# Mixture of experts: a fixed order on TensorE, nested conditions for further blocks, one hinted jump

## The chip, the cores and the metric

The kernel runs on one core of a Trainium2 chip. The metric is the device time of one execution in microseconds (us). The engines are TensorE (PE in the rows; its weight loads are PEld), VectorE (DVE), ScalarE (ACT), GpSimd (POOL) and SyncE (SP), which here only issues DMAs. A "q" behind an engine's name means its sequencer: the part that waits, branches and issues.

## What is computed

Two layers of a transformer block: a mixer (RWKV, S5 and windowed attention), a layer norm, a mixture of experts, a layer norm. The change touches the mixture of experts alone:

```python
def hier_moe(h, ...):                       # h: 768 tokens in layer 1, 512 in layer 2, of 1024 features
    ...                                     # each token: a group, two of its 8 experts, two weights
def run_block(inp):                         # a block of tokens of one expert e
    x_blk, e = inp
    return (silu(x_blk @ w_gate[e]) * (x_blk @ w_up[e])) @ w_down[e]
```

There are 32 experts in each layer; w_gate and w_up are 1024 x 512, w_down is 512 x 1024, all in float32, so an expert has 6.29 MB of weights. All 32 are read in each layer, whatever their number of tokens.

## The kernel before

Routing writes a table of the tokens of each expert to DRAM. In `experts` (L1867) a static path takes each expert's first block of 64 tokens; `NB` (L1699) is 3, so a second and a third block stand behind a condition each, and a loop at the end takes what is beyond (L1902). `rt.nov` holds the number of further blocks of each expert.

`tokens_T` (L1734) turns the gathered rows of two experts at once into `xT`: 8 transposes on TensorE (line L59 in the rows, from `xg`, or `xo` for further blocks) and two copies. `ffn_up` (L1749) is the product with gate and the product with up, 16 matmuls each (a float32 matmul shows as two in the trace), then silu on ScalarE (L1758) and the product of both on VectorE (L1759), called `act`. `ffn_down` (L1763) turns `act` by two transposes (L59), copies the result to `aT` on VectorE (L1770), makes the product with down in 8 matmuls (L1775), empties the bank (L1777, on ScalarE in the first layer, on VectorE in the second, where a gate row is multiplied in), and scatters the rows to DRAM from GpSimd (L1778).

The loop is shifted by one: in turn e it makes `ffn_up` of expert e, then, if e is odd, `tokens_T` of the next pair and the gather for a later one, then `ffn_down` of expert c = e - 1, then the conditions of c (L1895). The order on each engine is a scheduler's, not written by hand. Each of the engines TensorE, VectorE, ScalarE and GpSimd reads the number n of c (L1893) and branches for itself; an engine that skips a block still sends the semaphores that the block would have sent.

`Weights` (L1786) keeps three experts' matrices in a ring. SyncE issues the three fetches of expert e + 3 (L1811) when TensorE has passed the conditions of expert e, since the further blocks read the same matrices. `others` (L1853) fetches the tokens of further blocks, under a condition on GpSimd.

Of the kernel before, what the change touches and what calls it, by code (L numbers as in the profile page):

```python
# [10 lines left out]
F32 = mybir.dt.float32  # L11
# [9 lines left out]
D = 1024  # L21
# [9 lines left out]
class K:  # L31
    """the state of the build: engines, pools, constants"""

    def __init__(self, tc, a):
        self.tc, self.nc, self.a = tc, tc.nc, a
        self.dr = {}
        self.win = {}               # split columns of w_in
        self.free = []              # streams to use once instead
        self.stream = ('m', 8)      # the PSUM banks of the code being traced: tag, number
# [6 lines left out]
    def bank(self):  # L46
        """a PSUM bank of the current stream"""
        return self.ps.tile([128, 512], F32, name='b_' + self.stream[0], tag='b_' + self.stream[0], bufs=self.stream[1])

    def pool(self, name, st, **kw):  # L50
        """a pool whose tiles wait for the earlier tiles on their own bytes only"""
        return st.enter_context(self.tc.tile_pool(name=name, bufs=1, reuse_waits="tile", **kw))


def tr(k, out, x):
    """out = x^T on the tensor engine"""
# [5 lines left out]
def row(ap):  # L62
    """a DRAM vector [n] as [1, n]"""
# [18 lines left out]
def rsqrt(k, out, x, eps, p=128):  # L82
    """out = (x + eps)^-0.5 for a small tile"""
# [7 lines left out]
def mod_c(k):  # L91
    """silu of both condition vectors, [128, 8, 32] with d = 8 p + k, columns 0 (lat) and 1 (ctx)"""
# [13 lines left out]
    # b_mod of the first two thirds in columns; shift and 1 + scale of both layers  # L106
# [7 lines left out]
def mod_unit(k, l, mp, c0, n, bufs=2):  # L114
    """columns c0..c0+n of the modulation: the first two vectors to k.cols, the other four as rows to DRAM, 512 columns at a time"""
# [31 lines left out]
# float32 operands of the projection are split exactly into two of the tensor engine's 22-bit floats: x = hi + lo  # L147
def x_turn(k, xr, i, x):
    """columns of token tile i of xr [128, 8, 768], d = 128 k + p, from x [128, 1024]"""
# [7 lines left out]
def x_split(k, l, xT, xr, kk):  # L157
    """rows kk of xT from xr: modulated, split"""
# [11 lines left out]
def ln_rows(k, l):  # L170
    """the affine map of layer l's second norm, feature-major"""
# [6 lines left out]
def ln_cols(k, l, P, gb):  # L178
    """in feature-major columns the affine map gb of layer l's second norm and the next layer's modulation together"""
# [10 lines left out]
def x_tile(k, l, P, xT, i, x, cols):  # L190
    """columns of token tile i of xT from x [128, 1024]: turned, and by what is returned scaled and shifted, split"""
# [22 lines left out]
def win(k, l, pp, at, load=False):  # L214
    """columns 256 at.. of w_in, split; or their load alone"""
# [14 lines left out]
def proj(k, l, pp, xT, sink, tiles, segs=SEGS):  # L230
    """sink(m, c0, psum, n) takes feature tile m (128 features) of n tokens from c0"""
# [18 lines left out]
def rwkv_consts(k):  # L250
    """triangular masks over blocks of 64 tokens, one per direction"""
    nc, c = k.nc, k.cp
    k.cum, k.msk = [], []
    for d in range(2):
        # cum[i, t] = -e^-0.5 where i comes no later than t in the same block
# [6 lines left out]
        # msk[i, (a, r), t]: strictly before, no later  # L262
# [17 lines left out]
def rwkv_weights(k, l, rp, fp):  # L280
    """fp: pool of what only the features take"""
    nc, a = k.nc, k.a
    wa = fp.tile([128, 2, 2, 256], F32, name='wa2')      # w2 and a2, each zero on the other's rows
# [25 lines left out]
def conv_sink(k, P, cv, cvd, m, c0, p, n):  # L309
    """cvd [tile, 128, 8, 128] <- the centred convolution of the feature rows in PSUM"""  # L310
# [8 lines left out]
def to_tiles(k, d, m, c0, n, o, eng=None):  # L319
    """d [tile, 128, m, 128] <- o [128, n], feature tile m, tokens c0..c0+n"""  # L320
# [4 lines left out]
def rwkv(k, l, st, cvd, Y, ys, streams, fill):  # L325
    """cvd [tile, 128, 8, 128] convolved features; ys gets the tiles of the mixer's output, in pool Y, feature-major [128, 2, 128].
    streams: two PSUM streams; fill traces other work between the parts"""
    nc, tc = k.nc, k.tc
    emit_ctx = l == 0
    P = k.pool('rwA', st)       # lives through the chain  # L330
    sS, sF = ExitStack(), ExitStack()
    Q = k.pool('rwS', sS, side='right')     # the inverses
    Fp = k.pool('rwF', sF)      # features and scores of the tiles
    Rp = None                   # the steps
    pb, wa, g2 = rwkv_weights(k, l, P, Fp)
    V, G, A = nc.vector, nc.gpsimd, nc.scalar
    # of the chunk c of tile slot s: what a step takes (kb | v, W | x a | r | scores of r), what the inverse takes (scores of a), a | A_ak v
# [4 lines left out]
    def sigmoid(t):  # L342
        """(1 + tanh(x / 2)) / 2"""
# [7 lines left out]
    inv_o = k.dram('inv_out', [96, 64, 64])     # zero off the diagonal blocks of 32  # L351
    inv_t = k.dram('inv_t', [96, 32, 32])

    # the triangular inverses go in two batches; in each the forward tiles first
# [4 lines left out]
    # v, zero on the rows of b; keys and b of each head of a pair, zero on the rows of the other head  # L359
# [7 lines left out]
    def front(i):  # L367
        """token-major features of tile i"""
# [5 lines left out]
        # the low-rank inputs: tanh(w_lo) | a_lo, the gate's  # L374
# [5 lines left out]
        # decay  # L380
# [5 lines left out]
        # learning rate  # L386
# [5 lines left out]
        rk = Fp.tile([128, 512], F32, name='rk', bufs=2)      # r | k  # L392
# [11 lines left out]
        # unit keys  # L404
# [12 lines left out]
        # the decay of a whole chunk, per key channel  # L417
# [7 lines left out]
        gm = P.tile([128, 8, 2], F32, name='gm%d' % i)        # (d, pair, chunk), head of the pair  # L425
        G.tensor_tensor(gm, gc[:, :, None].to_broadcast([128, 8, 2]), k.hpm[:, None, :].to_broadcast([128, 8, 2]), op=ALU.mult)
        GM[i] = (gc, gm)
        # keys of both directions
# [6 lines left out]
        # a = kk * decay up to the token before  # L435
# [8 lines left out]
        if out:  # L444
            # the bonus
# [11 lines left out]
        for d in range(2):  # L457
            z = slot[i, d]
            # keys and v above, b and W below
# [1776 lines left out]
```

## Time and profile before

| | us |
|---|---|
| three runs | 2976.47, 2986.68, 2986.15 |
| their median | 2986.15 |
| the profiled execution: span from first to last instruction | 2973.4 |
| experts of the first layer, first to last product | 936.2 to 1541.6 |
| experts of the second layer | 2373.4 to 2923.7 |

The profiled execution has no time of its own beside its span; the runs lie 3 to 13 us above it. A row of the profile gives the line, the engine, what is written from what, how often, the busy time, and in brackets the idle time of the engine just before and what ended it. "PEq L1895" as what ended it means that TensorE stood still while its sequencer was at the condition. [...]

### The profile page before, as it was taken

To read this page: it belongs to the slowest core of one execution; us is meant where nothing else is said; L and a number is where in the kernel's file an instruction comes from. 1 tells how busy PE (TensorE), PEld (TensorE's weight loads), DVE (VectorE), ACT (ScalarE), POOL (GpSimd) and SP (SyncE) were. 2 spreads that over 40 slices of the span, in tenths; PEclk is the share of its full clock that TensorE was granted. 3 is DMA by queue.
4 is the path that set the end of the run, shared out by engine and by line. 5 is a ranking of instruction groups with operands and counts; after the bars stand their busy time and mean duration, and the time that the engine had idled before them with its cause. 6 is when DMAs were issued, how large, how long until landed. Compare 5 with 4: busy or idle time off the path is not lost. (4 is left out here: it accounts for less than half of the span.)

```text
span 2973.4 us, 43762 instructions
## 1 busy us (share of the span) xinstructions
PE 2257.8 (76%) x16189; PEld 1533.3 (52%) x16189; DVE 1180.0 (40%) x2830; ACT 522.9 (18%) x1264; POOL 821.5 (28%) x1131
## 2 busy tenths in 40 slices
PE   5898676879775878888864788677797487788882
PEld 3786455667433544555434676455554254454441
DVE  7963455564754000000006873456646611111113
ACT  3222332222001000000014122233120100000001
POOL 2642232331633010111006552333334410011002
PEclk8999677599887999999987898689798699999996
DMA  8334466567547898788865324446783699979994
GB/s 233 94 93 127 141 179 177 152 175 200 178 161 276 337 418 355 307 333 328 328 247 178 83 54 134 116 127 165 222 237 122 258 372 398 390 316 357 365 403 162
DMA packets 404799, 691.40 MB, mean 233 GB/s; under 512 B 134754, under 2 KB 310626, under 8 KB 388096
## 3 DMA queue, kind: packets, MB, share of 16 engines
q1 hardware_dynamic: 311808, 600.10, 56.4%
q10 hardware_dynamic: 78880, 64.32, 7.2%
q0 software_dynamic: 13792, 22.61, 2.1%
q8 instruction: 215, 3.52, 0.5%
q14 instruction: 104, 0.85, 0.1%
HBM read 607.98 MB, written 95.44 MB: 237 GB/s over the span
## 5 line engine op out<-in xcount | busy, mean ns | idle before, releaser
L1756 PE MATMUL b_m<-w,xT 128*64 128x256 f32 x4928 | 605.3, 406 | 145.4 <-PEq L1895 120.2
L1756 PEld LDWEIGHTS b_m<-w,xT 128*64 128x64 f32 x4928 | 431.6, 146 | 340.0 <-issue 125.2
L1759 DVE TENSOR_TENSOR act<-act,b_m 128x256 f32<-128x256 f32 x64 | 26.9, 421 | 751.7 <-PE b_m L1756 751.7
L243 PE MATMUL b_m<-xT,win 128*128 128x256 f32 (+1 forms) x1416 | 273.6, 353 | 8.1 <-POOL xT L167 3.7
L1775 PE MATMUL b_m<-w,aT 128*64 128x512 f32 x1024 | 233.8, 598 | 36.0 <-issue 18.7
L243 PEld LDWEIGHTS b_m<-xT,win 128*128 128x128 f32 x1416 | 230.8, 200 | 41.6 <-POOL xT L167 4.5
L1778 POOL DMA_INDIRECT yb<-y,dx x64 | 63.9, 999 | 630.9 <-DVEq L1895 297.1
L1775 PEld LDWEIGHTS b_m<-w,aT 128*64 128x64 f32 x1024 | 74.3, 136 | 154.3 <-issue 130.1
L1758 ACT ACTIVATE act<-b_m 128x256 f32<-128x256 f32 x64 | 24.5, 383 | 586.3 <-PE b_m L1756 586.2
L877 PE MATMUL b_a<-kz,qb 128*128 128x128 f32 (+2 forms) x416 | 114.9, 423 | 8.6 <-ACT pr L898 5.8
L1582 PE MATMUL b_a<-wo,yt 128*128 128x512 f32 x240 | 112.3, 617 | 0.0
L1842 POOL DMA_INDIRECT xg<-hd,ix x32 | 32.6, 1020 | 248.4 <-PE b_m L59 187.5
L877 PEld LDWEIGHTS b_a<-kz,qb 128*128 128x128 f32 x416 | 79.3, 240 | 32.9 <-issue 13.6
L127 PE MATMUL b_a<-wmod,cc 128*32 128x128 f32 x1280 | 65.4, 320 | 40.1 <-DMA wmod<-in_w_mod_dram 29.9
L59 PE MATMUL b_a<-idf,pr 128*128 128x128 f32 x320 | 59.1, 307 | 35.8 <-DVE pt L921 11.6
L503 PE MATMUL b_g<-ar,bz 128*128 128x128 f32 (+1 forms) x384 | 69.2, 348 | 8.0 <-ACT bz L495 8.0
L503 PEld LDWEIGHTS b_g<-ar,bz 128*128 128x128 f32 x384 | 63.9, 255 | 18.7 <-ACT bz L495 14.6
L1582 PEld LDWEIGHTS b_a<-wo,yt 128*128 128x128 f32 x240 | 45.3, 196 | 51.2 <-issue 50.3
L1777 DVE TENSOR_TENSOR y<-b_m,gate 128x512 f32<-128x512 f32 x32 | 22.1, 691 | 120.8 <-PE b_m L1775 120.8
L127 PEld LDWEIGHTS b_a<-wmod,cc 128*32 128x32 f32 x1280 | 38.3, 123 | 58.2 <-DMA wmod<-in_w_mod_dram 32.7
L551 POOL TENSOR_TENSOR tl<-Bm,Xh 112x4 f32<-112x4 f32 (+13 forms) x112 | 37.8, 337 | 103.0 <-DVE Xh L552 58.9
L59 PEld LDWEIGHTS b_a<-idf,pr 128*128 128x128 f32 x320 | 38.8, 154 | 45.3 <-DVE pt L921 13.7
(539 smaller groups left out, 3967.7 us busy)
## 6 DMA issues: line engine op xcount, KB each, us to landing
w<-in_expert_w_gate_dram SPq DMA_DIRECT2D x64, 2048.0 KB
w<-in_expert_w_up_dram SPq DMA_DIRECT2D x64, 2048.0 KB
w<-in_expert_w_down_dram SPq DMA_DIRECT2D x64, 2048.0 KB
wmod<-in_w_mod_dram SPq DMA_DIRECT2D x80, 512.0 KB
rec<-rec SPq DMA_DIRECT2D x40, 512.0 KB
win<-in_w_in_dram SPq DMA_DIRECT2D x16, 1024.0 KB
wmod<-in_w_mod_dram SPq DMA_DIRECT2D x4, 2048.0 KB
sca<-sc SPq DMA_DIRECT2D x24, 256.0 KB
```

Source lines behind the costliest of these rows:

```text
L59: k.nc.tensor.transpose(out, x, k.idf[r:r + n, r:r + n])
L127: nc.tensor.matmul(p[32 * g:32 * g + 32, :], k.cc[:, kk, :], wt[:, kk, :], start=kk < 4, stop=kk >= 4, tile_position=(0, 32 * g))
L243: nc.tensor.matmul(p[:, :n], wt[u][:, kk, j * 128:j * 128 + 128], xT[v][:, kk, c0:c0 + n], start=kk == 0 and q == 0, stop=kk == 7 and q == 2)
L503: nc.tensor.matmul(pv[:, cp, q, 0:n, :], bk[:, hp, q, cp].rearrange("p s t -> p (s t)"), ar[:, 0:n, cp, q, :], start=True, stop=True)
L551: eng.tensor_tensor(t[:, 0:n, j:32], Bm[:, r0:r1, j:j + 1].to_broadcast([112, n, w]), x.to_broadcast([112, n, w]), op=ALU.mult)
L877: nc.tensor.matmul(dst, qb[:, 2 * v + e, :], kz[:, v, r, 128 * keys[c][0]:128 * keys[f - 1][0] + 128], start=c == 0 or (c == 4 and r == 0) ...
L1582: nc.tensor.matmul(ps[h], y[:, kt, :], wo[:, kt, 512 * h:512 * h + 512], start=kt == 0, stop=kt == 5)
L1756: nc.tensor.matmul(p[64 * h:64 * h + 64, 0:256], xT[:, kk, :], w[:, kk, 256 * h:256 * h + 256], start=kk == 0, stop=kk == 7)
L1759: nc.vector.tensor_tensor(a, a, pu[:, 0:256], op=ALU.mult)
L1775: mm = nc.tensor.matmul(py[64 * s:64 * s + 64, :], aT[:, j, 64 * h:64 * h + 64], wd[:, q, 512 * s:512 * s + 512], start=q == 0, stop=q == 3)
L1778: sc = nc.gpsimd.indirect_dma_start(out=yb, out_offset=bass.IndirectOffsetOnAxis(ap=dst, axis=0), in_=y, in_offset=None, bounds_check=3071 ...
L1842: return nc.gpsimd.indirect_dma_start(out=out, out_offset=None, in_=hd, in_offset=bass.IndirectOffsetOnAxis(ap=idx, axis=0), bounds_check= ...
```

## The change

`ffn_down` loses its first part, the turn of `act`, to a new function `ffn_turn`. `ffn_up` gets a list of functions that are called between the product with gate and the product with up. In the loop these are: a branch hint for the condition of c, the turn of `act` of c, and for odd e the tokens of the next pair and the gather. The number n of c is read at the head of the turn, no longer behind the down product. The conditions are nested: the third block's stands inside the second block's, so an expert without further blocks meets one condition, which jumps over both. TensorE's order is the order of the code (`manual_schedule`); the other engines stay with the scheduler. Comments are removed throughout, which the diff leaves out here.

```diff
-def ffn_up(k, M, xT, wg, wu, more=''):
+def ffn_up(k, M, xT, wg, wu, more='', between=()):
     nc = k.nc
-    pg, pu = k.bank(), k.bank()
-    for p, w in ((pg, wg), (pu, wu)):
+    pg, pu = k.bank(), None
+    for w in (wg, wu):
+        if w is wu:
+            for f in between:
+                f(mm)
+            pu = k.bank()
+        p = pg if w is wg else pu
         for kk in range(8):
             for h in range(2):
-                nc.tensor.matmul(...)
+                mm = nc.tensor.matmul(...)
...
+def ffn_turn(k, M, a, more=''):
+    pa = k.bank()
+    for j in range(2):
+        tr(k, pa[:, 128 * j:128 * j + 128], a[:, 128 * j:128 * j + 128])
+    aT = M.tile([128, 2, 128], F32, name='aT' + more, bufs=1 if more else 2)
+    k.nc.vector.tensor_copy(aT, pa[:, 0:256].rearrange("p (j x) -> p j x", j=2))
+    return aT
...
-    act = {}
-    for e in range(NE + 1):
-        if e < NE:
-            w = wts.get(e)
-            act[e] = ffn_up(k, M, xT[e // 2][:, :, 64 * (e % 2):64 * (e % 2) + 64], w[0], w[1])
-            if e % 2 and e + 1 < NE:
-                j = (e + 1) // 2
-                xT[j] = tokens_T(k, M, xg[j % AHEAD])
-                first(j + AHEAD - 1)
-        if e == 0:
-            continue
-        c = e - 1
-        w = wts.get(c)
-        with ExitStack() as late:
-            for x in ffn_down(k, M, act.pop(c), w[2], rt.dx[:, 0, c:c + 1], yb, gate):
-                late.enter_context(tc.issue_after(x.ins))
-            n = nc.values_load(rt.nov[0:1, c:c + 1], min_val=0, max_val=11, engines=k.engs)
-        for b in range(1, NB):
-            with tc.If(n > b - 1):
-                x2 = tokens_T(k, M, more(c // 2, b)[64 * (c % 2):64 * (c % 2) + 64])
-                ffn_down(k, M, ffn_up(k, M, x2, w[0], w[1], 'o'), w[2], rt.dx[:, b, c:c + 1], yb, gate, 'o')
-        if c % 2:
-            others(c // 2 + 1, 2)
-            others(c // 2 + 2, 1)
+    act, aT = {}, {}
+
+    def turned(c):
+        aT[c] = ffn_turn(k, M, act.pop(c))
+
+    def hint(c, mm):
+        with tc.issue_after(mm.ins):
+            tc.mark_branch_hint_location('beyond%d_%d_1' % (l, c), hint='LikelyTaken', engines=[ET.PE])
+
+    def tokens(j):
+        xT[j] = tokens_T(k, M, xg[j % AHEAD])
+        first(j + AHEAD - 1)
+
+    def beyond(c, w, n, b):
+        if b == NB:
+            return
+        with tc.If(n > b - 1, label='beyond%d_%d_%d' % (l, c, b) if b == 1 else None):
+            x2 = tokens_T(k, M, more(c // 2, b)[64 * (c % 2):64 * (c % 2) + 64])
+            x2 = ffn_turn(k, M, ffn_up(k, M, x2, w[0], w[1], 'o'), 'o')
+            ffn_down(k, M, x2, w[2], rt.dx[:, b, c:c + 1], yb, gate, 'o')
+            beyond(c, w, n, b + 1)
+
+    with tc.manual_schedule(engines={ET.PE}):
+        for e in range(NE + 1):
+            c = e - 1
+            if c >= 0:
+                n = nc.values_load(rt.nov[0:1, c:c + 1], min_val=0, max_val=11, engines=k.engs)
+            between = [lambda mm: hint(c, mm), lambda mm: turned(c)] if c >= 0 else []
+            if e < NE:
+                w = wts.get(e)
+                if e % 2 and e + 1 < NE:
+                    between.append(lambda mm: tokens((e + 1) // 2))
+                act[e] = ffn_up(k, M, xT[e // 2][:, :, 64 * (e % 2):64 * (e % 2) + 64], w[0], w[1], between=between)
+            else:
+                turned(c)
+            if c < 0:
+                continue
+            w = wts.get(c)
+            ffn_down(k, M, aT.pop(c), w[2], rt.dx[:, 0, c:c + 1], yb, gate)
+            beyond(c, w, n, 1)
+            if c % 2:
+                others(c // 2 + 1, 2)
+                others(c // 2 + 2, 1)
```

What this does to TensorE's order, at the third expert of the first layer (x16 counts matmuls of one product; w_8505 and w_8507 are its gate and up, w_8072 is the second expert's down). Before:

```order
L1756 MATMUL b_m<-w_8505,xT_8317 64x256 x16
L1756 MATMUL b_m<-w_8507,xT_8317 64x256 x16
L59 MATMUL b_m<-idf,act 128x128 x2
L1775 MATMUL b_m<-w_8072,aT 64x512 x8
L1893 TENSOR_LOAD nov
L1893 ISA x2
L1895 COMPARE_AND_BRANCH
```

On TensorE at the same place, now (the third expert's gate and up are w_8521 and w_8523 here):

```order
L1917 TENSOR_LOAD nov
L1917 ISA x2
L1762 MATMUL b_m<-w_8521,xT_8318 64x256 x16
L2266 BRANCH_PREFETCH_HINT
L59 MATMUL b_m<-idf,act 128x128 x2
L1762 MATMUL b_m<-w_8523,xT_8318 64x256 x16
L1786 MATMUL b_m<-w_8072,aT 64x512 x8
L1907 COMPARE_AND_BRANCH
```

The reading of n went from behind the down product to the head, the hint and the two transposes of `act` went between the two products, and the branch follows the down product directly.

On VectorE at the same place, before (the rows between the two branches are the second block):

```order
L1759 TENSOR_TENSOR act<-act,b_m 128x256
L1770 COPY aT<-b_m 128x256
L1893 TENSOR_LOAD nov
L1895 COMPARE_AND_BRANCH
L1745 COPY xT_8581<-b_m 128x256
L1759 TENSOR_TENSOR acto<-acto,b_m 128x256
L1770 COPY aTo<-b_m 128x256
L1895 UNCONDITIONAL_BRANCH x2
L1856 UNCONDITIONAL_BRANCH
L1895 COMPARE_AND_BRANCH
```

On VectorE, now:

```order
L1775 COPY aT<-b_m 128x256
L1765 TENSOR_TENSOR act<-act,b_m 128x256
L1917 TENSOR_LOAD nov
L1907 COMPARE_AND_BRANCH
L1745 COPY xT_8585<-b_m 128x256
L1765 TENSOR_TENSOR acto<-acto,b_m 128x256
L1775 COPY aTo<-b_m 128x256
L1907 COMPARE_AND_BRANCH
```

The copy of the older expert's turned activation went ahead of the newer expert's product, and the second condition follows the second block's work inside the first.

## Rows read from the trace of the kernel before

**Rows 1.** Windows of both expert stretches: stretch, us, busy by engine, PEclk, DMA share, GB/s.
```profile
936.00:1542.00 606.00, 507.89 (x3556) 307.07 (x3554) 47.19 (x107) 53.38 (x108) 61.71 (x62) 0.96 0.83 333
2373.00:2924.00 551.00, 449.96 (x3107) 268.82 (x3105) 65.34 (x128) 25.94 (x57) 52.42 (x52) 0.94 0.90 361
```
**Rows 2.** TensorE's waits, first stretch: engine, line, releaser: us in total, times, longest.
```profile
PE b_m L1756 <- PEq L1895: 60.0, 27, 4.0
PE b_m L1775 <- issue: 9.7, 16, 0.6
PE b_m L1775 <- DVE aT L1770: 8.3, 16, 0.5
...
PE b_m L1756 <- issue: 5.4, 5, 1.5
```
**Rows 3.** TensorE's waits in the second stretch.
```profile
PE b_m L1756 <- PEq L1895: 60.2, 21, 4.3
PE b_m L1756 <- issue: 9.2, 5, 3.2
...
PE b_m L1756 <- DMA w<-in_expert_w_gate_dram: 1.0, 1, 1.0
```
**Rows 4.** Timeline of TensorE: start us, us, instruction, count [idle before, releaser].
```profile
1092.70 3.65 PE L1775 MATMUL b_m<-w,aT 128*64 128x512 f32 x16 [0.52 <-DVE aT L1770]
1099.97 8.81 PE L1756 MATMUL b_m<-w,xT 128*64 128x256 f32 x64 [3.61 <-PEq L1895]
...
1113.34 1.09 PE L59 MATMUL b_m<-idf,xo 64*128 64x64 f32 x8
...
1123.28 3.65 PE L1775 MATMUL b_m<-w,aTo 128*64 128x512 f32 x16 [0.52 <-DVEq L1895]
1127.25 7.13 PE L1756 MATMUL b_m<-w,xT 128*64 128x256 f32 x64 [0.31 <-PEq L1895]
...
1264.02 7.13 PE L1756 MATMUL b_m<-w,xT 128*64 128x256 f32 x64 [0.31 <-PEq L1895]
...
1276.54 7.85 PE L1756 MATMUL b_m<-w,xT 128*64 128x256 f32 x64 [0.77 <-ACTq L1895]
```
**Rows 5.** Windows behind one long pause, columns as in rows 1.
```profile
1099.90:1103.30 3.40, 3.33 (x16) 2.34 (x18) 0.00 (x0) 0.00 (x0) 0.00 (x0) 0.53 1.03 398
1103.60:1108.70 5.10, 5.10 (x48) 3.79 (x44) 0.00 (x0) 0.38 (x1) 0.00 (x0) 1.00 1.03 435
```
**Rows 6.** TensorE's sequencer at the condition, three passages: min/median/max ns, starts; the number's load.
```profile
L1895 PEldq COMPARE_BRANCH  x2: 323/1709/3095, 1093.5 to 1096.6; - x2
L1895 PEldq EVENT_SEMAPHORE  x2: 51/51/51, 1096.4 to 1099.7; - x2
...
L1895 PEldq COMPARE_BRANCH  x2: 222/324/425, 1137.0 to 1140.1; - x2
...
L1895 PEldq COMPARE_BRANCH  x2: 219/2657/5095, 1151.5 to 1156.8; - x2
...
L1893 PEldq TENSOR_LOAD <-nov x1: 305/305/305, 1092.8 to 1092.8; - x1
```
**Rows 7.** First stretch: SyncE's wait (us, times, longest); the instruction queue's packets, MB, share.
```profile
SPq L1811 <- PEq L1895: 477.0, 28, 26.9
...
q8 instruction: 68, 1.11, 0.7%
```
**Rows 8.** Window in which the weights' ring is behind, columns as in rows 1.
```profile
1040.00:1080.00 40.00, 31.52 (x208) 18.42 (x204) 3.02 (x7) 3.11 (x6) 4.53 (x5) 0.96 1.01 421
```
**Rows 9.** Groups by line, both stretches: count, busy us, mean ns, idle before.
```profile
L1777 ACT COPY y<-b_m 128x512 f32<-128x512 f32 x32 | 18.7, 585 | 189.7 <-PE b_m L1775 119.1 <-PEq L1895 70.6
...
L1775 PE MATMUL b_m<-w,aTo 128*64 128x512 f32 x144 | 32.9, 599 | 4.6 <-DVEq L1895 3.6 <-DVE aTo L1770 1.0
...
L1775 PE MATMUL b_m<-w,aTo 128*64 128x512 f32 x64 | 14.6, 598 | 2.1 <-DVE aTo L1770 2.1
```

More of the change, by code (lines that the diff above doesn't have):

```diff
@@ L1746, in tokens_T @@
     return xT
-def ffn_up(k, M, xT, wg, wu, more=''):
+def ffn_up(k, M, xT, wg, wu, more='', between=()):
     nc = k.nc
-    pg, pu = k.bank(), k.bank()
-    for p, w in ((pg, wg), (pu, wu)):
+    pg, pu = k.bank(), None
[5 more added lines that the diff above has]
+        p = pg if w is wg else pu
         for kk in range(8):
             for h in range(2):
-                nc.tensor.matmul(p[64 * h:64 * h + 64, 0:256], xT[:, kk, :], w[:, kk, 256 * h:256 * h + 256], start=kk == 0, stop=kk == 7)
+                mm = nc.tensor.matmul(p[64 * h:64 * h + 64, 0:256], xT[:, kk, :], w[:, kk, 256 * h:256 * h + 256], start=kk == 0, stop=kk == 7)
     a = M.tile([128, 256], F32, name='act' + more, bufs=1 if more else 2)
@@ L1760, in ffn_up @@
     return a
-def ffn_down(k, M, a, wd, dst, yb, gate, more=''):
-    nc = k.nc
+def ffn_turn(k, M, a, more=''):
     pa = k.bank()
@@ L1769, in ffn_down @@
     aT = M.tile([128, 2, 128], F32, name='aT' + more, bufs=1 if more else 2)
-    cp = nc.vector.tensor_copy(aT, pa[:, 0:256].rearrange("p (j x) -> p j x", j=2))
+    k.nc.vector.tensor_copy(aT, pa[:, 0:256].rearrange("p (j x) -> p j x", j=2))
+    return aT
+def ffn_down(k, M, aT, wd, dst, yb, gate, more=''):
+    nc = k.nc
     py = k.bank()
@@ L1774, in ffn_down @@
         for s in range(2):
-            mm = nc.tensor.matmul(py[64 * s:64 * s + 64, :], aT[:, j, 64 * h:64 * h + 64], wd[:, q, 512 * s:512 * s + 512], start=q == 0, stop=q == 3)
+            nc.tensor.matmul(py[64 * s:64 * s + 64, :], aT[:, j, 64 * h:64 * h + 64], wd[:, q, 512 * s:512 * s + 512], start=q == 0, stop=q == 3)
     y = M.tile([128, 512], F32, name='y' + more, bufs=2 if more else 3)
-    ev = nc.scalar.copy(y, py) if gate is None else nc.vector.tensor_tensor(y, py, gate, op=ALU.mult)
+    if gate is None:
+        nc.scalar.copy(y, py)
+    else:
+        nc.vector.tensor_tensor(y, py, gate, op=ALU.mult)
     sc = nc.gpsimd.indirect_dma_start(out=yb, out_offset=bass.IndirectOffsetOnAxis(ap=dst, axis=0), in_=y, in_offset=None,
@@ L1782, in ffn_down @@
     k.tc.add_to_no_dep_group(yb.tensor.name, sc.ins)
-    return mm, cp, ev, sc
 class Weights:
@@ new lines, in experts @@
+    with tc.manual_schedule(engines={ET.PE}):
[9 more added lines that the diff above has]
+                act[e] = ffn_up(k, M, xT[e // 2][:, :, 64 * (e % 2):64 * (e % 2) + 64], w[0], w[1], between=between)
+            else:
+                turned(c)
[7 more added lines that the diff above has]
+                others(c // 2 + 2, 1)
@@ L1916, in experts @@
             x2 = tokens_T(k, M, xg[0][0:64])
-            ffn_down(k, M, ffn_up(k, M, x2, w[0], w[1], 'o'), w[2], di, yb, gate, 'o')
+            x2 = ffn_turn(k, M, ffn_up(k, M, x2, w[0], w[1], 'o'), 'o')
+            ffn_down(k, M, x2, w[2], di, yb, gate, 'o')
 def combine(k, l, P, w, yb, x1, put):
```

## The prediction

> **What bounds the kernel now.** I read the windows of the two stretches in which the experts run first [rows 1]: 605.3 us in the first layer (first product at 936.2, last at 1541.6) and 550.3 us in the second (2373.4 to 2923.7), together 39% of the span of 2973.4. TensorE is busy for 508 and 450 us of them and the DMA engines for 83% and 90%, so neither fills either stretch. The waits say why TensorE pauses: it waits for its own sequencer at the condition (L1895) before the next expert's products, 60.0 us in 27 cases and 60.2 us in 21 [rows 2, 3]. Almost no row says that a weight came late (1.0 us once, in rows 3).
>
> The timeline shows one expert of each sort [rows 4]. At 1099.97 the products with gate and up start 3.61 us after the end of the down product and take 8.81 us; at 1127.25 and 1264.02, after 0.31 us, they take 7.13. [...] So a slow passage costs some 5 us, a quick one (0.77 us before 1276.54) next to nothing.
>
> What the pause is made of stands in the sequencer's rows [rows 6]. An expert without further blocks takes two jumps, one over the second block's code and one over the third's. Before 1099.97 the first took 0.32 us, the second 3.10; for the next but one expert (1137.0 and 1140.1) both were short. The first is read while the down product still runs (it starts at 1093.5, the product ends at 1096.35), so its price is covered. The second stands behind a semaphore that is sent when the product has ended (1096.4), so its price is paid in full. In the long case a block of code is fetched: the queue of instructions moved 68 packets, 1.11 MB (16 KB each) in this stretch [rows 7].
> [...]
>
> The weights set the second limit. An expert's three matrices of 2 MB go into a ring of three experts, and SyncE issues the next when TensorE has passed the old one's condition: 477.0 us of waits, 28 of them [rows 7]. When the ring is behind, the DMA engines are full (share 1.01, 421 GB/s, of which about 400 are weights [rows 8]): 6.29 MB / 0.40 = 15.7 us an expert. In the rest of the time they idle because the release came late.
>
> **The change, part by part.**
> *Nested conditions.* One jump over both blocks in place of two. It is read while the down product runs, as the first jump is now; there is no second. That takes away the exposed 2.8 us (3.61 less 0.77) and the slow clock behind it. The one jump is twice as long, so its target will lie more often in code that is not there: bounds 0.3 and 3.1 us, once 5.1 (rows 6, third answer). Of that some 2.9 us are hidden by the product (1093.5 to 1096.4), leaving 0 to 2.2 us; I take 0.1, the row of 3.1 being nearest.
> *The number read at the head.* TENSOR_LOAD (L1893) took 0.31 us, and from its start to the branch 0.7 passed (1092.8 to 1093.5 [rows 6]), beside the down product. Now they stand between two experts and are exposed. ScalarE, or VectorE in the second layer, has to empty the down product's bank meanwhile (585 ns on ScalarE [rows 9]) and to pass the condition, which takes as long, so the two lie beside each other. I take a gap of 1.2 us: 0.77 less its last branch of 0.43, plus 0.7, plus 0.1.
> *Turns between gate and up.* The transposes of the activation no longer wait for it, and its copy on VectorE lies under the product with up. That saves the 0.52 to 0.60 us before each down product (9.7 + 8.3 us in rows 2). The next tokens' transposes only move: 1.16 us per pair of experts as before, and the gather that follows them on GpSimd is for a pair two further on; I cost it at nothing. If that cover failed, the waits of 0.6 would come back, 38 us in all.
> *The hint.* One instruction on TensorE's sequencer, issued while the product with gate runs; I cost it at nothing. What it does to the fetch is not in this trace: from taking away all of a hidden fetch (0) to putting one fetch of 3.1 us in the way of each skip. It is wrong for the 11 experts (8 and 3, counted along the timeline) that have further blocks; at 3.1 us each that is 0 to 34 us.
> *Moved instructions.* SyncE's three fetches of an expert keep their place behind the release, which now comes 0.3 us after the down product. VectorE turns the order of two operations round (copy of the old activation ahead of the new product); both inputs are there earlier, so nothing waits. All else of the program stays.
>
> **The sum.** TensorE's time per expert becomes 7.13 + 0.44 + 0.58 + 3.65 + 1.2 = 13.0 us. A further block costs 13.6 (1113.34 to 1126.93 [rows 4]); there are 9 and 4, from 144 and 64 down matmuls at 16 each [rows 9]. With 1.5 us for the slow first product TensorE alone would need 537 us (24 plain experts and 8 with blocks) and 471 us.
> Then I walk both lists against the ring: expert e+3 is fetched after the release of e, at 15.8 us an expert in the first layer (more tokens move) and 15.6 in the second, and each product starts at the later of TensorE's time and its matrix's landing. The same walk with the old order, and the pauses as traced, ends at 1539.5 and 2923.7 (traced 1541.6 and 2923.7). With the new one TensorE waits 7 us for weights in the first layer, where extra blocks let the ring fill, and some 30 in the second, where experts 4 to 14 run at the DMA's pace; the stretches take 548 and 510 us. That is 57 and 40 us less. I take off 9 for code that arrives late in straight runs too (the waits put down to "issue", 5.4 and 9.2 us [rows 2, 3]) and for wrong hints: 88 us.
> The profiled span of 2973.4 becomes 2885. The three runs took 2976.5, 2986.2 and 2986.7 us, so their median lies 12.8 above the span; with the same margin the time is **2898 us**.
> [...]
>
> **The rivals.**
> *The hint does nothing and jumps are partly exposed.* The target of the double jump is missing more often, and the fetch begins so late, or lasts so long (5.1 us in rows 6), that the gap is 2.0 to 2.5 us. The walk then gives 566 and 516 us (2.0) or 586 and 523 (2.5): 75 or 47 us gained, 2911 to 2939, about 2925. For it: one of the three passages shown has a fetch that long. Against: the others fit under the product.
> *The weights are the bound anyway.* The DMA share is 0.90 in the second layer already; were that stretch held by the DMA alone, only the first would gain, and with 16.3 us an expert in place of 15.8 the walk gives it 50 us: 2936. Against: TensorE waits for weights in one row only, and SyncE waits for TensorE.
> *Slower: the hinted block pushes out code that runs next.* Place: between the hint and the condition, where the block fetched ahead would lie. Each hit costs 3.1 us and 1.7 of clock. Over all 24 and 29 plain experts that is 537 + 115 and 471 + 139 us, 652 and 610, 107 us more than now; at 6 in 10 of them it is even, at 8 in 10 it is 57 us slower: 3043. For it: a second fetch, soon after a first, is what the long second jump shows now. Against: the way from hint to condition is short beside a block.
> *No change.* The same displacement in half to six tenths of the experts, or a pause for another engine's passage of the condition that is as long as the old one: about 2980.
>
> **How the numbers follow.** The forecast 0.60, hint without effect 0.18, weights 0.06, slower 0.10, no change 0.06. The predicted time is the first's. Its own range is 2878 (gap 0.8, no deduction) to 2915; the range for 8 in 10 reaches into the next two, 2868 to 2948. About 0.5% (15 us) is what a measurement of this kernel can tell from no change. Faster by more: 0.60 + 0.18 + 0.06 = 0.84; within: 0.06; slower: 0.10.
>
> **What would show it.** Right: the condition's branch on TensorE's sequencer once per plain expert, begun before the down product's end; the pause before the next gate product 1.0 to 1.4 us; gate and up at 7.1 us plus waits in between; no 0.5 us before the down product; DMA share above 0.95 over most of the second layer, with TensorE now waiting for weights there. Wrong: pauses of 3 us that stay, now behind one jump or inside a product (the hint), or stretches that shrink in one layer alone (the weights).

## The result, and the profile after

The changed kernel takes 2899.4 us (median of five runs, 2883.0 to 2907.2) where the kernel before takes 2986.2 (five runs, 2976.5 to 2992.1): 0.971 of it, with an interval of 0.968 to 0.975. The forecast was 2898. The sum is right, and two of the steps that lead to it are wrong; the experiments show which.

The profiled execution has a span of 2881.2 us and took 2883.0. Its windows over the two expert stretches (columns as in rows 1) answer to [rows 1]:

```profile
929.80:1484.70 554.90, 488.92 (x3555) 285.22 (x3554) 48.90 (x106) 53.22 (x107) 61.84 (x62) 0.98 0.90 363
2312.40:2831.80 519.40, 438.28 (x3105) 252.72 (x3104) 66.36 (x126) 25.99 (x57) 52.52 (x52) 0.96 0.94 383
```

From first product to last they are 554.8 and 519.4 us long, in place of 605.4 and 550.2: 50.6 and 30.8 us less. The other 10.8 us by which the span of 2973.4 shrinks lie outside them (1807.0 us in place of 1817.8). The program there is the same, and in ten of the kernels below that share it the rest takes 1810 to 1835 us: it differs from run to run by more than 10.8, and I don't put these to the change.

TensorE's waits of the first stretch (us in total, times, longest) answer to [rows 2]:

```profile
PE b_m L1762 <- DMA w<-in_expert_w_gate_dram: 24.4, 9, 5.8
PE b_m L1762 <- ACTq L1907: 12.7, 10, 1.8
PE b_m L1762 <- PEq L1907: 6.4, 6, 1.3
PE b_m L1762 <- issue: 6.4, 6, 1.3
...
PE b_m L1762 <- DMA w<-in_expert_w_up_dram: 2.6, 4, 1.3
```

and of the second stretch, to [rows 3]:

```profile
PE b_m L1762 <- DMA w<-in_expert_w_gate_dram: 55.8, 18, 4.5
PE b_m L1762 <- DVEq L1907: 12.9, 11, 1.4
PE b_m L1762 <- DMA w<-in_expert_w_up_dram: 4.6, 7, 1.5
```

The 60.0 and 60.2 us behind TensorE's own sequencer are 6.4 and nothing. In their place weights are waited for, 27.0 and 60.4 us: the wait that was one row of 1.0 us in [rows 3] is now the largest of both stretches. The waits of 0.5 to 0.6 us ahead of each down product have gone.

The timeline of TensorE (start, us, instruction, count, idle before and its releaser) shows the new order beside [rows 4]:

```profile
1082.95 5.55 PE L1762 MATMUL b_m<-w,xT 128*64 128x256 f32 x32 [5.82 <-DMA w<-in_expert_w_gate_dram]
1088.43 0.44 PE L59 MATMUL b_m<-idf,act 128*128 128x128 f32 x2
1088.80 3.67 PE L1762 MATMUL b_m<-w,xT 128*64 128x256 f32 x32
1092.31 3.60 PE L1786 MATMUL b_m<-w,aT 128*64 128x512 f32 x16
1095.84 1.09 PE L59 MATMUL b_m<-idf,xo 64*128 64x64 f32 x8
...
1119.16 3.60 PE L1786 MATMUL b_m<-w,aT 128*64 128x512 f32 x16
1123.77 3.67 PE L1762 MATMUL b_m<-w,xT 128*64 128x256 f32 x32 [1.00 <-PEq L1907]
1127.37 0.44 PE L59 MATMUL b_m<-idf,act 128*128 128x128 f32 x2
1127.74 3.67 PE L1762 MATMUL b_m<-w,xT 128*64 128x256 f32 x32
```

Gate, turn (the two products with idf and act), up and down follow each other without a gap. The pause before the next gate product is 1.00 us at 1123.77, where no weight is late. At 1082.95 it is 5.82, for a weight, and the gate product then takes 5.55 us in place of 3.67. The windows of that product and of one behind a pause of 1.36 us (at 1110.79) show why: the granted clock (third number from the end, a share of full speed) is 0.65 against 1.00, as the 8.81 us in [rows 4] go with the 0.53 in [rows 5]:

```profile
1082.90:1088.50 5.60, 5.55 (x33) 3.46 (x34) 0.00 (x0) 0.00 (x0) 0.00 (x0) 0.65 1.01 412
1110.80:1114.40 3.60, 3.60 (x33) 2.61 (x33) 0.00 (x0) 0.00 (x0) 1.56 (x2) 1.00 0.80 323
```

The jumps themselves, all of TensorE's passages of the condition (min/median/max ns, first and last start), first stretch and second:

```profile
L1907 PEldq COMPARE_BRANCH  x49: 70/360/4736, 946.3 to 1481.2; - x49
...
L1907 PEldq COMPARE_BRANCH  x39: 70/761/5186, 2328.8 to 2828.2; - x39
```

Long ones are still there, as in the window 1129 to 1135:

```profile
L1907 PEldq COMPARE_BRANCH  x1: 3537/3537/3537, 1130.8 to 1130.8; - x1
```

This one ends at 1134.4, ahead of the end of the down product (1134.85), and so costs nothing.

### The profile page after: what moved, and what is told of

It reads as the page before. It is cut to its first block, busy times and chain, and to the rows that moved or that the text cites. A ratio compares the mean times of both kernels' runs of the same rounds, so it can differ in the third digit from the quotient of the medians.

```text
span 2881.2 us, 43454 instructions
## 1 busy us (share of the span) xinstructions
PE 2219.2 (77%) x16189; PEld 1487.5 (52%) x16189; DVE 1185.8 (41%) x2830; ACT 523.3 (18%) x1264; POOL 823.0 (29%) x1131
## 5 line engine op out<-in xcount | busy, mean ns | idle before, releaser
L1762 PE MATMUL b_m<-w,xT 128*64 128x256 f32 x4928 | 593.7, 396 | 128.8 <-DMA w<-in_expert_w_gate_dram 80.2
L1762 PEld LDWEIGHTS b_m<-w,xT 128*64 128x64 f32 x4928 | 391.9, 142 | 333.3 <-issue 148.0
L1775 DVE COPY aT<-b_m 128x256 f32<-128x256 f32 x64 | 27.2, 425 | 474.4 <-PE b_m L59 474.4
L1792 POOL DMA_INDIRECT yb<-yo,dx x13 | 12.9, 994 | 291.7 <-ACTq L1907 166.2
```

Source lines behind the costliest of these rows:

```text
L1762: mm = nc.tensor.matmul(p[64 * h:64 * h + 64, 0:256], xT[:, kk, :], w[:, kk, 256 * h:256 * h + 256], start=kk == 0, stop=kk == 7)
L1775: k.nc.vector.tensor_copy(aT, pa[:, 0:256].rearrange("p (j x) -> p j x", j=2))
L1792: sc = nc.gpsimd.indirect_dma_start(out=yb, out_offset=bass.IndirectOffsetOnAxis(ap=dst, axis=0), in_=y, in_offset=None, bounds_check=3071 ...
```

## The experiments

One table holds what they measured. "Stretches" are first to last product of the experts in the profiled run. They are of one profiled run for each kernel, and how far they differ from run to run of one kernel is not on record: differences of a few us there are indications, not more. "Jumps" is the time of all taken jumps of the 52 or 53 experts that skip their further blocks (with some 2 us for a short last jump of each of the 11 others), and in brackets how many are over 4.5 us; it is summed from the records of TensorE's sequencer. The ratios stand against runs of the kernel before on the same chip.

| kernel | ratio (interval) | stretches, us | sum | jumps, us |
|---|---|---|---|---|
| before | 1 | 605.4 + 550.2 | 1155.6 | 124.7 (1) |
| nesting alone | 0.996 (0.994 to 0.998) | 604.6 + 547.9 | 1152.5 | 211.1 (29) |
| nesting and hint | 0.976 (0.971 to 0.981) | 567.8 + 526.7 | 1094.5 | 74.3 (5) |
| changed kernel | 0.971 (0.968 to 0.975) | 554.8 + 519.4 | 1074.2 | 116.5 (4) |
| without the hint | 0.982 (0.978 to 0.986) | 583.3 + 522.8 | 1106.1 | 230.4 (29) |
| conditions not nested | 0.996 (0.994 to 0.998) | 605.2 + 540.3 | 1145.5 | 129.8 (7) |
| hint earlier | 0.970 (0.966 to 0.975) | 554.1 + 520.8 | 1074.9 | 92.5 (4) |
| turns late | 0.981 (0.976 to 0.986) | 574.9 + 527.6 | 1102.5 | 71.5 (4) |
| number at the tail | 0.968 (0.963 to 0.973) | 546.4 + 517.2 | 1063.6 | 87.5 (0) |
| number between | 0.973 (0.969 to 0.977) | 561.4 + 519.9 | 1081.3 | 150.9 (14) |
| no fixed order | 0.974 (0.969 to 0.978) | 552.7 + 516.8 | 1069.5 | 117.7 (4) |
| half of the weights | one run | 529.5 + 457.5 | 987.0 | 96.5 (2) |
| two pieces | 0.969 (0.965 to 0.973) | 550.3 + 518.0 | 1068.3 | 113.9 (5) |
| best parts together | 0.963 (0.960 to 0.967) | 536.9 + 516.1 | 1053.0 | 73.8 (0) |

### The hint taken away

```diff
-            between = [lambda mm: hint(c, mm), lambda mm: turned(c)] if c >= 0 else []
+            between = [lambda mm: turned(c)] if c >= 0 else []
```

> The changed kernel without its hint, all else kept. My theory: the jump is read some 4 us before the down product ends and is hidden there with or without a hint, so nothing changes: within 0.5% of the changed kernel's 2899 us (0.971 of before), stretches of 555 and 519 us, and the jumps that take 2.5 to 5 us are as many as with the hint. Rival 1, the hint fetches the target ahead: without it more jumps are long and outlast the product, half of 53 skips by 0.5 to 1.5 us, 13 to 40 us slower than the changed kernel. Rival 2, the hint puts fetches in the way: without it 10 to 30 us faster.

2925.6 us: 26 above the changed kernel's median, and 32 us more in the stretches. My theory falls, and the first rival holds, more strongly than it said. The jumps of the first and second stretch, to be held against the same rows of the changed kernel (the median of the first is small in both, since half of its 49 passages are of experts with further blocks):

```profile
L1907 PEldq COMPARE_BRANCH  x49: 65/373/6646, 955.2 to 1518.6; - x49
...
L1907 PEldq COMPARE_BRANCH  x39: 65/3167/6791, 2368.3 to 2871.3; - x39
```

The median of the second is 3.17 us in place of 0.76. Of the 52 jumps that skip, 29 last over 4.5 us, most of them 5.8 to 6.8, where the changed kernel has 4. A jump of 6.6 us that starts 4.0 us ahead of the down product's end sticks out by 2.6, and the median pause is 2.9 us.

### Nesting alone

```diff
+        def beyond(b):
+            if b == NB:
+                return
+            with tc.If(n > b - 1):
...
+                beyond(b + 1)
+        beyond(1)
-        for b in range(1, NB):
-            with tc.If(n > b - 1):
```

> The kernel before with its two conditions nested, nothing else changed. My theory: the exposed second jump (2.8 us and 1.7 of slow clock) goes from the plain experts, while 0.5 us before each down product stay and the number is still read behind the product: 55 to 80 us below before, 2905 to 2930. Rival, nesting only makes the one jump longer or moves the fetch, and the turns or the hint brought the gain: within 0.5% of before.

The stretches are as long as before (604.6 and 547.9), and the time is 0.4% less (0.2 to 0.6%). This takes away the base of my forecast: the exposed second jump is gone, and its time is not. One passage, in the rows of the timeline, of the condition and of the DMA queue of instructions (packets, MB, share) in the window 1085.6 to 1088.3:

```profile
1088.63 8.81 PE L1756 MATMUL b_m<-w,xT 128*64 128x256 f32 x64 [3.56 <-PEq L1897]
...
L1897 PEldq COMPARE_BRANCH  x1: 6027/6027/6027, 1082.2 to 1082.2; - x1
...
q8 instruction: 1, 0.02, 2.5%
```

The one jump starts at 1082.2 and lasts 6.0 us. The queue q8 moved nothing from 1082.1 to 1085.6; its one packet of 16 KB starts at 1085.7, 3.5 us after the jump, and 1.4 us after its end the jump is done and TensorE goes on. Now the passage of [rows 6] in the kernel before again. From 1093.4 to 1097.1 q8 moved nothing there, and from 1097.1 to 1098.4:

```profile
q8 instruction: 1, 0.02, 5.3%
```

The first jump was at 1093.5 and the second ended at 1099.7, 6.2 us later. So the packet comes 3.7 us after the *first* jump, and over all 28 such passages of the kernel before the medians are 3.7 us from the first jump to the packet and 6.1 us to the end of the second. The 3.1 us of the second jump were the rest of a fetch of 6.1 us that the first one had set off. Nesting adds up the two, and the pause stays.

### Nesting and the hint, nothing else

```diff
+        if hint and w is wu:
+            hint(mm)                      # behind the last product with gate
```

> The kernel before with its conditions nested and the jump hinted, the turns and the number's read where they were before. My theory after the runs without the hint and with nesting alone: nesting makes one jump of some 6 us out of two of 0.3 and 3.1, the hint takes its first 3 us away, and the remaining 3.1 us begin 2.9 us before the down product's end, so the pause falls from 3.4 to about 1.0 us: stretches of 565 to 580 and 520 to 535 us, 45 to 70 us below before, 2910 to 2935. Rival, the hint only helps a jump that is read 4 us ahead, with the number already there: pauses stay above 2.5 us and the time within 1% of before.

2910.9 us, 0.976, stretches 567.8 and 526.7: my corrected theory holds, and the hint does more than it said. Most jumps take 0.35 us. One passage, from the hint (L2243) over the jump (L1904) to the next gate product, and q8 in the window 1038.0 to 1039.5:

```profile
L2243 PEldq BRANCH_PREFETCH_HINT  x2: 36/36/36, 1034.2 to 1046.7; - x2
...
q8 instruction: 1, 0.02, 4.5%
...
L1904 PEldq COMPARE_BRANCH  x1: 424/424/424, 1040.1 to 1040.1; - x1
...
1043.73 2.16 PE L1758 MATMUL b_m<-w,xT 128*64 128x256 f32 x17 [0.77 <-ACTq L1904]
```

The hint is at 1034.2, the packet starts at 1038.1, 3.9 us behind it, and the jump at 1040.1 finds its target there and takes 0.42 us. The packet follows the hint much as it follows a jump without a hint (3.5 us in the passage above, 3.7 in the median before), and it is there before the jump, so the hint sets the fetch off. Not always: four jumps of this kernel still take 6.0 to 6.4 us, with the packet 3.6 to 3.9 us behind the jump as if there were no hint; why is not known. The number of packets in the two stretches is no larger (65 + 65 here, 68 + 67 with nesting alone): the hint moves fetches, it adds none.

### The conditions one behind the other, hint kept

```diff
-            beyond(c, w, n, b + 1)
...
-            beyond(c, w, n, 1)
+            for b in range(1, NB):
+                beyond(c, w, n, b)
```

> The changed kernel with its two conditions one behind the other again, the hint, the turns and the number's place kept: the nesting alone is undone. My theory: the second jump stands behind a semaphore sent at the down product's end again and is paid in full where it misses (3.1 us and 1.7 of slow clock, in about half of 53 skips, part of it swallowed by waits for weights in the second layer): 45 to 90 us above the changed kernel, 2945 to 2990. Rival, the gain came from the moved turns and the hint: less than 15 us above it.

0.996, stretches 605.2 and 540.3, 71 us more than in the changed kernel: in the range of my theory. The waits behind the sequencer are back, first stretch and second:

```profile
PE b_m L1762 <- PEq L1907: 53.9, 16, 8.1
...
PE b_m L1762 <- PEq L1907: 62.8, 18, 7.3
```

With the hint on the first condition the first jumps of the second stretch take 0.2 to 2.0 us, and 13 of its 28 second ones still 1.8 to 2.6, behind the product's end. In these 13 the packet starts 3.5 to 4.3 us after the first jump: as in the kernel before, the second shows the rest of a fetch that began at the first, and four others take 3.5 to 6.1 us. So neither the nesting nor the hint works without the other: one hint names one of two targets, and with nesting alone the one jump has the whole fetch.

### The hint earlier

```diff
-        with tc.issue_after(mm.ins):      # mm: the last product with gate
+        with tc.issue_after(mm.ins):      # mm: the second product with gate
```

> The changed kernel with the hint behind the first two products with gate instead of the last: some 3 us earlier, 9 to 10 us ahead of the jump in place of 6 to 7. My theory: the hint itself starts the fetch of the target, whose packet starts 4 to 5 us after it and needs 2.5 more until the jump can pass; so with the longer lead most jumps that fetch (17 of 2.8 us and more, 5 over 4) shrink to 0.4 us. Since all but a few are hidden under the down product already, the time changes little: 0 to 12 us below the changed kernel. Rival, the hint only readies the queue and the packet waits for the jump itself: jumps stay at about 3 us. Second rival, an earlier hint is overtaken by the ordinary fetch of the next page and lost: jumps of 6 us return, 15 us or more above the changed kernel.

Jumps fall from 116.5 to 92.5 us and the time stays (0.970), as my theory says of the time; of the jumps it promised more. The median lead from hint to jump grew from 6.6 to 8.0 us only, since the sequencer issues ahead of the products (in the changed kernel the hint behind the gate product that ends at 1127.4 runs at 1125.1). In five kernels the jumps get shorter with a longer lead, up to some 8 us: 116.5 us at a median of 6.6 us (the changed kernel), 87.5 at 7.3 (number at the tail), 71.5 at 8.0 (turns late), 74.3 at 8.4 (nesting and hint), 73.8 at 9.5 (best parts together). This kernel with 92.5 at 8.0, the half of the weights with 96.5 at 6.0 and the number between with 150.9 at 6.6 don't lie on that line: the lead is not all that counts. In the changed kernel the packet comes 3.5 to 5.6 us after the hint in 23 of 50 passages, whose jumps have a median of 0.9 us, and mostly 6 to 9 us after it in the other 27 (3.1 us). Why it comes late there was not found: some of these have another packet of q8 in between, most have not. (The queue moves packets in code without a jump too: 15 packets of 16 KB in the first 400 us of the changed kernel, where no engine branches.)

### The turns late

```diff
-            between = [lambda mm: hint(c, mm), lambda mm: turned(c)] if c >= 0 else []
+            between = [lambda mm: hint(c, mm)] if c >= 0 else []
...
+            turned(c)                     # behind the up product
```

> The changed kernel with the activation's transposes behind the up product again, just ahead of the down product: hint, nesting and number kept. My theory: the wait of 0.52 to 0.60 us for the copy comes back before each down product, 17 to 19 us on TensorE in each stretch; in the first layer most of it counts, in the second half is swallowed by waits for weights: 15 to 28 us above the changed kernel. Rival, with weights the bound in both stretches the turns are hidden: less than 8 us.

2925.7 us, 28 us more in the stretches (20.1 + 8.2): the upper end of my theory. The waits before the down products, first stretch and second, are those of [rows 2, 3] again:

```profile
PE b_m L1786 <- issue: 9.5, 16, 0.6
...
PE b_m L1786 <- DVE aT L1775: 8.9, 16, 0.6
...
PE b_m L1786 <- DVE aT L1775: 17.8, 32, 0.6
```

### The number's place, three times

Behind the start of the down product, as before the change:

```diff
-                n = nc.values_load(rt.nov[0:1, c:c + 1], ...)           # at the head
+                for x in ffn_down(...): late.enter_context(tc.issue_after(x.ins))
+                n = nc.values_load(rt.nov[0:1, c:c + 1], ...)
```

> The changed kernel with the number of further blocks read behind the start of the down product again; hint, nesting and turns kept. My theory: the jump begins 1.1 us later, 2.9 us before the product's end, and sticks out by 0.2 us or more where it fetches, while TENSOR_LOAD and its register work (0.7 us) leave the pause: the pause is 0.5 us where nothing is fetched and 0.8 to 1.3 where it is; within 0.5% of the changed kernel. Rival, what counts is the 4 us of lead that the early number gives: pauses of 1.5 us and more, 15 to 40 us slower than the changed kernel.

0.968, and 10.6 us less in the stretches: by these, the number at the head costs a little. The jump starts 3.3 us ahead of the product's end in place of 4.0, but the hint has 0.7 us more (a median of 7.3 us for 6.6) and the jumps are shorter (87.5 us for 116.5), and the load no longer stands in the pause, here 0.56 us:

```profile
1410.93 3.67 PE L1762 MATMUL b_m<-w,xT 128*64 128x256 f32 x32 [0.56 <-PEq L1908]
```

By the times alone it is not shown: the intervals overlap (0.963 to 0.973 and 0.968 to 0.975).

Between the gate and up products, behind the hint:

```diff
-                n = nc.values_load(rt.nov[0:1, c:c + 1], ...)           # at the head
-            between = [lambda mm: hint(c, mm), lambda mm: turned(c)] if c >= 0 else []
+            between = [lambda mm: hint(c, mm), lambda mm: number(c), lambda mm: turned(c)] if c >= 0 else []
```

> The changed kernel with the number read between the gate and up products, all else kept: the jump still begins 4 us before the down product's end, and the load no longer stands in the pause. My theory: pauses that do not wait for weights fall from 1.1 to about 0.6 us, 0.45 us for some 50 experts on TensorE; half of it comes back as waits for weights: 8 to 18 us below the changed kernel. Rival, the pause is another engine's passage (ScalarE's or VectorE's) and the load lies beside it: within 4 us of the changed kernel.

No gain, 7.1 us more in the stretches: pauses that wait for no weight are shorter in the first stretch (ScalarE's 7.6 us for 12.7), but jumps take 150.9 us in place of 116.5, and 14 of them over 4.5. Neither my theory nor the rival has that; why a load right behind the hint goes with longer jumps stays open.

And with the fixed order on TensorE taken away, which leaves the products in their sequence but puts all 32 reads of a layer ahead of its first expert:

```diff
-    with tc.manual_schedule(engines={ET.PE}):
+    with ExitStack():
```

> The changed kernel without the fixed TensorE order: the products stay in the same sequence, but all 32 numbers of a layer are read in a row ahead of the first expert. My theory: a read takes TensorE's sequencer about 0.7 us (0.30 of TENSOR_LOAD, 0.15 of register work and what lies between), so some 22 us stand ahead of the first expert in each layer, while the pauses fall from 1.1 to 0.5 us, which weights let through only in part (8 us and 2 us in the stretches): 20 to 40 us above the changed kernel, 2920 to 2940. Rival, the reads lie beside the last of the routing or the first weights' landing: 5 to 15 us below the changed kernel.

0.974, as the changed kernel: a miss. The 32 reads take 23 us (920.2 to 943.2), but from the routing's last counts to the first expert's product 28.1 us pass in place of 19.5, since TensorE waits there for VectorE in the changed kernel too (12.2 us before 922.7); and the stretches are 4.7 us shorter. What the fixed order buys by itself is too small to measure here.

### Half of the weights

```diff
-        f = nc.sync.dma_start(v, s)
+        f = nc.sync.dma_start(v[:, 0:z], s[:, 0:z])     # z: half of the tile
...
-                mm = nc.tensor.matmul(..., w[:, kk, 256 * h:256 * h + 256], ...)
+                mm = nc.tensor.matmul(..., w[:, kk % 4, 256 * h:256 * h + 256], ...)
```

> The changed kernel, with only the first half of each expert matrix fetched (1 MB in place of 2) and the products run on that half twice: the work of TensorE is the same, the transfers are half, the numbers computed are others. My theory: my miss of 7 and 9 us in the stretches is waiting for weights (27 and 60 us in place of 7 and 30): with half the bytes no wait for a weight is left and the stretches are 515 to 537 and 455 to 475 us. Rival, TensorE's own pauses are longer than I summed (code, gaps over 1.2 us) and weights are hidden anyway: stretches above 545 and 505.

The windows of its stretches:

```profile
934.70:1464.30 529.60, 480.85 (x3555) 276.96 (x3554) 48.91 (x107) 53.12 (x107) 61.97 (x62) 0.99 0.54 201
2307.30:2764.90 457.60, 417.84 (x3105) 240.71 (x3104) 66.33 (x127) 25.93 (x57) 52.39 (x52) 1.00 0.61 227
```

529.5 and 457.5 us, with no wait for a weight left and a clock of 0.99 and 1.00: my theory holds. This is the time of TensorE with its pauses alone, so weights cost the changed kernel 25.3 and 61.9 us.

### Two pieces

```diff
+        nc.sync.dma_start(v[:, 0:z], s[:, 0:z])
+        nc.sync.dma_start(v[:, z:], s[:, z:])
-        nc.sync.dma_start(v, s)
```

> The changed kernel with every expert matrix fetched in two transfers of 1 MB, all else kept. My theory: where TensorE waits for weights, a product can start when the first half has landed, some 2.6 us earlier, and that lead is kept when an expert with further blocks follows: 5 to 15 us below the changed kernel, stretches of 543 to 553 and 508 to 517 us. Rival, at 400 GB/s the transfers run back to back and set the pace whatever their size: the same stretches within 3 us, with the waits only moved into the middle of the products, and time within 0.3%.

5.9 us less in the stretches (4.5 + 1.4), inside the stretch of my theory in the first, and in the second outside it and within the rival's 3 us; the times overlap (0.969 and 0.971), so no gain is shown. The weights' queue in the window 2360 to 2440, where the ring is behind, in the changed kernel and in this one (packets, MB, share):

```profile
q1 hardware_dynamic: 4273, 32.39, 97.8%
```

```profile
q1 hardware_dynamic: 5681, 32.05, 98.1%
```

32.39 MB in 80 us are 405 GB/s, with the engines' share at 97.8%, and 98.1% in pieces of 1 MB: there the transfers set the pace in both.

### The best parts together

The changed kernel with three of the edits above:

```diff
+        with tc.issue_after(mm.ins):      # the hint behind the second product with gate
...
+                n = nc.values_load(rt.nov[0:1, c:c + 1], ...)           # at the tail
...
+        nc.sync.dma_start(v[:, z:], s[:, z:])                           # the second piece
```

> A version put together from the runs: nested conditions, turns between the products, the hint behind the first gate products, the number read behind the start of the down product, and every matrix fetched in two transfers. My theory: the parts add, as far as weights allow: 15 to 30 us below the changed kernel, 2870 to 2885, stretches of 535 to 545 and 505 to 515 us. Rival, weights are the floor and no part but the first counts: 2885 to 2900.

2870.6 us (2866.9 to 2876.7), 0.963: faster than both kernels, by 0.8% against the changed one going by the ratios, and the interval ends (0.967) where that of the changed kernel begins (0.968). The first stretch is at 536.9, near the 529.5 that TensorE took on half of the weights (there with the number at the head); the second at 516.1, just outside the range expected, is still held by the weights (52.7 us of waits for gate and up, a DMA share of 0.96). Which of the three parts brings how much is not shown.

## Why the prediction was right, and where it was not

**The exposed second jump.** The step "so its price is covered. The second stands behind a semaphore [...] so its price is paid in full" failed. The fetch begins at the first jump and takes 6.1 us, the second shows what is left of it. The rows of [rows 6 and 7] held this: two jumps 3.1 us apart, and a second one long only by what 6.1 less 3.1 leaves. With that, "leaving 0 to 2.2 us; I take 0.1" could not stand, nor did the target of the longer jump lie more often in code that is not there (29 jumps of over 4.5 us with nesting alone; before, 28 such passages and one jump of 5.1): nesting alone left all of the pause and gained 3.1 us in the stretches where I counted most of 97.

**The hint.** "I cost it at nothing" failed too, in the other direction: with all else as changed it is worth 32 us in the stretches, with nesting alone 58. Its bounds (0 to a loss of 3.1 us) had no gain on the path in them, because I held the fetch for hidden. The two errors meet in the same pause and cancel: nesting and hint together take away what I gave to nesting. That is why the sum came out, and it is luck: the mechanism was right only for the pair. The rival in which the hint does nothing had 2911 to 2939, about 2925, and the kernel without the hint takes 2925.6: its price was right, its chance should have hung on a hint of which no row told anything.

**The wrong hints.** Almost no price: the next tokens' products of an expert with a further block follow the down product at once, as at 1095.84. Of the 0 to 34 us it was some 1.3: the 13 further blocks take 178.2 us in sum, 176.9 without the hint, and the difference is one block of 14.9 us in place of 13.6, at the second layer's expert with two of them:

```profile
2584.28 1.09 PE L59 MATMUL b_m<-idf,xo 64*128 64x64 f32 x8
2585.58 5.37 PE L1762 MATMUL b_m<-w,xT 128*64 128x256 f32 x47 [0.20 <-DVE xT L1745]
2591.86 2.16 PE L1762 MATMUL b_m<-w,xT 128*64 128x256 f32 x17 [0.91 <-issue]
```

Between the hint (2574.5) and this block q8 brings one packet (2579.0); the next starts at 2589.2 and lasts 1.0 us, and the products go on 1.6 us behind it. All nine hinted, nested kernels with whole weights have one such block, of 14.4 to 16.4 us; nesting alone and the changed kernel without the hint have none. So the wait for code that the slower rival feared is seen once among the 11 wrong hints, and not over the plain experts as it had it; that the hinted code displaced the block's own is not shown.

**The number at the head.** I took a pause of 1.2 us; it is 1.0 to 1.4 where no weight is late, once 1.8 behind a jump of 4.7. The place cost 10.6 us in the stretches of the profiled runs against the number at the tail, which I had not set beside it.

**The turns.** 0.52 to 0.60 us for each expert; undone, they cost 20.1 and 8.2 us. In the first stretch that is the 18 of [rows 2] and a little more, in the second the weights take half of it.

**TensorE alone against the weights.** Here two terms are mis-sized, again against each other. TensorE alone was to need 537 and 471 us; half of the weights gives 529.5 and 457.5. Its plain experts take 12.1 and 13.1 us in turn (with the next tokens' transposes), 12.6 in the mean and not 13.0. Weights were to add 11 and 39 us; they add 25.3 and 61.9. Where the ring is behind, nine experts in a row take 14.5 to 16.7 us, mean 16.0, in the second stretch, in place of 15.6, and 11 of the 12 waits of over 3 us are paid a second time by the slow clock behind them (gate products of 5.0 to 6.3 us at a granted clock of 0.58 to 0.72, for 3.67 at 1.00), as are four of 2.3 to 2.9 us (5.4 us at 0.68). So the stretches are 554.8 and 519.4 in place of 548 and 510, and 81 us are gained there, where I had 97 less a reserve of 9. (The waits put down to "issue" in [rows 2, 3] were for code as I took them: each of the ten ends 2.2 to 2.5 us behind the start of a packet of q8.)

**The frame.** The profiled run lies 1.8 us under its time, and the median of the five 16.4 above that: the 12.8 us that I added are within what the runs differ by. In parts, the stretches came out 7 us above the 1067 that I had with the reserve, the rest 10.8 below, and the median lies 18.2 above the span in place of 12.8. That 2898 is met within 2 us is luck. (In the first rival, 566 and 516 us make 73.6 us gained and not 75.)

## What to carry to other kernels

A stall that is seen at an instruction may have begun at an earlier one, as the 3.1 us of the second jump here: follow the transfer back to what set it off before you price the removal of the last instruction in the row. The jumps were shortest here (71.5 to 74.3 us in sum) with one target in place of two and the hint 8.0 to 9.5 us ahead of it, though 92.5 us were also seen at 8.0: read that lead, and the packet behind the hint, in the trace of your own kernel. And when pauses go, ask how far the next limit is: of 169 us between the stretches before and TensorE's need alone, half came as gain and half was held back by the weights.

## What the runs showed that I had not expected

- A taken jump that fetched its target took mostly 5.8 to 6.8 us (nesting alone, and without the hint): 3.4 to 4.3 us until the packet of 16 KB started, 0.9 to 1.1 for it, 1.4 to 1.5 until TensorE went on.
- A hint of 0.04 us on TensorE's sequencer set off that fetch: the packet started 3.5 to 5.6 us behind it in 23 of 50 passages of the changed kernel and 27 of 50 with nesting and hint alone. In seven of those 23 the jump began 2.2 us or more behind the packet's start, and it took 0.35 to 0.47 us.
- A hint that named the wrong way cost nothing in 12 of 13 further blocks and some 1.3 us in one.
